# RWKV-7 head pairs in a two-layer hybrid backbone: the products of a pair made one stage later, with its solve and merge written ahead of the next pair's preparation

## The chip, the cores and the metric

The kernel runs on one core of one Trainium2 chip. The metric is the device time of one execution in microseconds; lower is better. A core has five engines that work side by side, each through its own list of instructions in order: PE (matrix products; its weight loads are shown apart, as PEld), DVE (vector), ACT (scalar), POOL and SP, the last two here mostly for issuing DMAs. They wait for each other by semaphores.

## The reference

Two layers over 512 latent tokens of width 1024, with 256 context tokens in front. The even layer runs a bidirectional RWKV-7 recurrence over 16 heads of width 64, side by side with a gated short convolution; the odd layer is a Conformer convolution module. What matters here is the recurrence, run once forward and once backward over the context and, from the states that this leaves, over the latent tokens:

```python
def step(S, inp):
    r_t, w_t, k_t, v_t, kk_t, a_t = inp
    sa = jnp.einsum("bhvk,bhk->bhv", S, -kk_t)
    S = (S * w_t[:, :, None, :]
         + sa[..., None] * (kk_t * a_t)[:, :, None, :]
         + v_t[..., None] * k_t[:, :, None, :])
    return S, jnp.einsum("bhvk,bhk->bhv", S, r_t)
...
out_f, S_f = wkv_scan(S0_f, rt, tm(decay[0]), tm(kd[0]), vt, kkt, tm(a[0]), False)
out_b, S_b = wkv_scan(S0_b, rt, tm(decay[1]), tm(kd[1]), vt, kkt, tm(a[1]), True)
```

Its output is normalised per head, a bonus term is added, and it is gated by SiLU of a projection. The short convolution is `bg * dwconv(cg * xb)`, gated as well. Both go through one output projection.

## The kernel before

Everything is float32; dense products are three float32r products of high and low parts (`mm3`, all recorded on L57). The heads are worked in eight pairs, 128 channels each. Time is cut into chunks of 64 tokens, four for the context and eight for the latent part, and the recurrence inside a chunk is turned into small matrices. For one pair (a state `st`) there are these pieces of work:

- `prep_lat` (P) loads the pair's k, v and r rows, which earlier projections left in device memory.
- `light` (L) forms decays and scaled vectors: a normalisation (`ss`, L479 to L489, with a reciprocal root of twelve tiny DVE instructions), and for each direction z a low-rank product on PE, tanh and exponentials on ACT, and the tiles AR and BK on DVE (L525 to L560). It uses the work tiles kd, a and P.
- `heavy` (H) makes the products of BK and AR on PE (`pal`, four groups of eight, each pair of banks masked into the tile E on DVE, L610), transposes BK (`pbl`), copies a part of E into `Nt` on ACT (L629), and copies v into UV (`pvl`, L640). The first product of a group waits until the group before has left its banks.
- `solve` (S) inverts the triangular blocks of E: it transposes `Nt` into X (L661), loads a unit matrix into Y, and makes 31 eliminations of two DVE instructions each (L667 and L669, tiles `xtmpl` and `Yl`).
- `merge` (M) puts the half-size inverses together: two transpositions on DVE (L675, L676), a copy into E (L680), a set of small products on PE (`uh`), a copy (L689), a second set, and a copy into E (L694). Its three work areas R1, R2 and Gs are taken from the tiles kd, a and P.
- the chain, `chain_lat`, walks the eight chunks. A step is a round trip: products of the state H with AR and of E with UV (`zol`) on PE, a copy on ACT (L769), a product with the inverse (`uh`), a copy into UV on ACT (L775), a product with BKt (`uh`), and the new state `Hl` on DVE (L782). The last of the eight steps makes no new state, so a pair has seven, `Hl_0` to `Hl_6`.
- `finish` (F) normalises a pair's output (`orq`, `po`) and stores it. `conv_branch` (C) makes the short convolution of another pair: four dense projections `pcg`, `pxb`, `pbg`, `pzb` of 24 products each, every one ahead of a weight cast on ACT and the low part on DVE (L129). The gate needs all of `pzb` and a tanh on ACT (L802).

The main loop goes over 12 stages: stages 0 to 3 run the chains of the context, stages 4 to 11 those of latent pairs 0 to 7. In every stage the chain of state s is written first, and then the letters of the table `STAGE` in their order. A letter works on the next state (O, S, M) or on the one after it (P, L, H). In the table before, the latent stages do O, S, P, L, M, H, F, C: `heavy` of a pair is written two stages ahead of its chain, its solve and merge one stage ahead, behind the next `light` for the merge.

The written order isn't the order of issue. The program goes through a scheduler that takes, among the instructions that its own time model calls ready, those written first; so work that stands later fills waits of the chain. `anchored` keeps pieces of `light` and `heavy` behind certain steps of the chain (`LIGHT_AFTER`, `HEAVY_AFTER`), and `conv_branch` has anchors of its own. The result is a fixed list per engine.

Of the kernel before, what the change touches and what calls it, by code (L numbers as in the profile page):

```python
# [15 lines left out]
P = 128  # L16
# [15 lines left out]
CONV_AFTER = (0, 2, 7, 6)  # L32
PA_ORDER = ((0, 1), (1, 0), (1, 1), (0, 0))
HEAVY = ("BAN", "ANBV")
STAGE = ("KLSMHVvF", "OPLSMHF", "OSPLMHFC")
FILL_R = (0, 0, 2, 3, 4, 4, 4, 4)
FILL_Z = (0, 1, 1, 1, 3, 3, 3, 3)
ZR = (slice(0, 64), slice(64, 128))
# [13 lines left out]
def kernel(ctx: ExitStack, tc: tile.TileContext, I: dict, out: bass.AP):  # L52
# [128 lines left out]
    def w(tag, name, dt=F32):  # L181
        return wk.tile([P, SIZE.get(tag, 512)], dt, tag=tag, name=name, bufs=NBUF.get(tag, 1))
# [470 lines left out]
    def solve(st):  # L653
        nm, E = st["nm"], st["E"]
        Xt = w("X", "X" + nm)
        X = Xt.rearrange("p (a b) -> p a b", b=32)
        Yt = w("Y", "Y" + nm)
        Y = Yt.rearrange("p (a b) -> p a b", b=16)
        tmp = w("xtmp", "xtmp" + nm)
        nc.gpsimd.dma_start(Y, I["unit"])  # L660
        V.transpose(X.rearrange("p (r s) t -> p t r s", r=2),  # L661
                    Nt.rearrange("p q t -> p t q").unsqueeze(2).to_broadcast([P, 32, 2, 16]))
        for i in range(31, 0, -1):
            c0 = i // 2
            m = 16 - c0
            tv = tmp[:, : i * m].rearrange("p (a b) -> p a b", b=m)
            V.tensor_tensor(out=tv, in0=X[:, :i, i : i + 1].to_broadcast([P, i, m]),  # L667
                            in1=Y[:, i : i + 1, c0:].to_broadcast([P, i, m]), op=ALU.mult)
            V.tensor_tensor(out=Y[:, :i, c0:], in0=Y[:, :i, c0:], in1=tv, op=ALU.add)  # L669
        st["Y"] = Y  # L670

    def merge(st):
        nm, E, Y = st["nm"], st["E"], st["Y"]
        R1, R2, Gs = (w(t, f"{t}m{nm}")[:, 0:512].rearrange("p (a b) -> p a b", b=32) for t in ("kd", "a", "P"))
        V.transpose(R1.rearrange("p q (c r) -> p c r q", r=2), Y.rearrange("p (a b) c -> p c a b", a=2))  # L675
        V.transpose(R2, R1)  # L676
        for z in range(2):
# [238 lines left out]
    sts = [prep_ctx(0, rest)]  # L916
# [15 lines left out]
    for s in range(12):  # L932
        st = sts[s]
# [7 lines left out]
            finish(st)  # L941
            break
        env["first"] = s < 4
        for x in STAGE[(s >= 2) + (s >= 4)]:
            if x == "S":
                solve(sts[s + 1])
            elif x == "M":
# [13 lines left out]
                light(sts[s + 2], st)  # L961
            elif x == "H" and s < 10:
                heavy(sts[s + 2], st)
            elif x == "F":
                fills(s + 1)
                if s >= 4:
# [47 lines left out]
    with ExitStack() as l1:  # L1014
# [182 lines left out]
        for j in range(16):  # L1197
# [5 lines left out]
            t = t2[:, j % 2 * 512 : j % 2 * 512 + 512]  # L1203
# [4 lines left out]
        for j in range(16):  # L1208
# [10 lines left out]
            t = lt("wb" if j < 10 else "xr", f"y{j}", F32R)  # L1219
# [129 lines left out]
```

## Time and profile before

| what | us |
|---|---|
| median of 3 runs (1419.38 to 1422.9) | 1421.06 |
| the profiled execution | 1428.73 |
| its span | 1426.4 |
| latent chains, first product of pair 0 to the end of pair 7 | 471.6 to 946.3 |
| from the first new state of pair 1 to that of pair 6 | 581.2 to 871.7 |

The page gives busy time per engine over the whole span; behind 946 us come the rest of the output projection and the odd layer. The stages in question are seen only by windows. A window row gives its length, then for PE, PEld, DVE, ACT and POOL the busy time with the number of instructions, the granted PE clock as a share of full speed, the share of DMA and GB/s. A row of a group gives line, engine, operation, out<-in, shapes and count, then busy time, mean ns of one, and idle time before it with what ended it. A row in the order of time gives start, length, engine, line, operation and, in brackets, the idle time before it.

### The profile page before, as it was taken

Reading aid. Unit: us, or ns where it says so; the run is one execution under the profiler, and the core shown is the slowest. Engines: PE = TensorE matmul, PEld = TensorE weight load, DVE = VectorE, ACT = ScalarE, POOL = GpSimd, SP = SyncE. Lnnn points to the kernel's source line nnn. Section 1 sums busy time; section 2 is a strip of 40 time slices with the busy share of each in tenths; the row PEclk is TensorE's granted clock in tenths of the full one; section 3 lists DMA queues with packets and bytes.
Section 4 is the critical chain, followed back from the end, with each engine's and each line's share of the span. In section 5 each row is a group of like instructions: output and inputs, shape, how many; then the busy total and the mean of one; then the engine's idle time right before and its main releaser. Section 6 shows DMA issues by size and latency. Waiting matters only on the chain.

```text
span 1426.4 us, 29742 instructions
## 1 busy us (share of the span) xinstructions
PE 1370.3 (96%) x11921; PEld 1002.7 (70%) x11921; DVE 982.2 (69%) x2294; ACT 748.5 (52%) x1516; POOL 118.2 (8%) x246
## 2 busy tenths in 40 slices
PE   6899999999999898999999999999999999999998
PEld 1474577787777676666676666768777777788886
DVE  2675597876898869999999998657745545544333
ACT  4635455535657555656666656456753323464322
POOL 2023210001011101011011100010000000000000
PEclk9999999889999999999999999999999999999999
DMA  9755432221232322232132212459813303133322
GB/s 322 226 180 160 143 121 82 64 89 59 90 101 71 112 77 68 70 100 67 56 90 70 85 47 88 130 166 323 261 40 117 119 18 101 59 104 89 103 89 89
DMA packets 137626, 158.54 MB, mean 111 GB/s; under 512 B 15375, under 2 KB 104143, under 8 KB 137369
## 3 DMA queue, kind: packets, MB, share of 16 engines
q1 hardware_dynamic: 121104, 106.47, 23.9%
q0 software_dynamic: 15312, 48.99, 10.7%
q8 instruction: 94, 1.54, 0.5%
q10 hardware_dynamic: 1072, 1.19, 0.2%
q14 instruction: 44, 0.36, 0.1%
HBM read 138.33 MB, written 18.28 MB: 110 GB/s over the span
## 4 chain that ended last, share of the span: by engine, by line
PE 52%; DVE 9%; ACT 4%; issue 2%; DMA 1%; POOL 0%; DVEq 0%; SPq 0%; ACTq 0%; POOLq 0%
PE pu L57 12%; PE pz L57 6%; PE f L57 6%; PE o L57 5%; PE zol L57 4%; PE pcg L57 3%; PE uh L57 3%; PE pxb L57 3%; DVE E L610 2%; PE pzb L57 1%; PE pc L57 1%; PE px L57 1%; PE pbg L57 1%; DVE Yl L669 1%; DVE xtmpl L667 1%
## 5 line engine op out<-in xcount | busy, mean ns | idle before, releaser
L57 PE MATMUL o<-wh,y 128*128 128x512 f32 x248 | 79.7, 397 | 0.0
L667 DVE TENSOR_TENSOR xtmpl<-Xl,Yl 128x126 f32<-128x126 f32 (+22 forms) x248 | 62.4, 252 | 3.0
L669 DVE TENSOR_TENSOR Yl<-Yl,xtmpl 128x126 f32<-128x126 f32 (+22 forms) x248 | 62.3, 251 | 2.9
L1162 ACT CAST ah<-a 64x512 fp32r<-64x512 f32 x32 | 19.8, 618 | 72.5 <-DVE a L1157 72.1
L57 PE MATMUL zol<-UV,E 64*64 64x64 f32 (+1 forms) x1024 | 54.0, 221 | 0.0
L57 PE MATMUL pal<-ARl,BKl 64*128 64x128 f32 x512 | 45.3, 296 | 7.7 <-DVE E L610 6.7
L57 PEld LDWEIGHTS o<-wh,y 128*128 128x128 f32 x248 | 45.9, 188 | 9.6
L57 PE MATMUL zol<-Hl,ARl 64*64 64x64 f32 x896 | 50.2, 230 | 1.1 <-DVE Hl L782 0.7
L775 ACT COPY UV<-uh 64x128 f32<-64x128 f32 x128 | 33.3, 260 | 32.7 <-PE uh L57 26.6
L57 PE MATMUL o<-wl,y 128*128 128x512 f32 x124 | 49.3, 398 | 0.7 <-DVE wl L129 0.7
L57 PEld LDWEIGHTS zol<-Hl,ARl 64*64 64x64 f32 x896 | 35.0, 133 | 21.3 <-issue 17.3
L57 PEld LDWEIGHTS pal<-ARl,BKl 64*128 64x128 f32 x512 | 35.6, 191 | 18.0 <-DVE E L610 6.8
L57 PEld LDWEIGHTS uh<-UV,BKt 128*64 128x64 f32 x704 | 26.3, 137 | 31.1 <-ACT UV L775 24.8
L129 DVE TENSOR_TENSOR wl<-wr,wh 128x1024 fp32r<-128x1024 f32 x28 | 34.2, 1223 | 20.2 <-ACT wh L128 20.0
L1157 DVE TENSOR_TENSOR a<-pu,a 128x512 f32<-128x512 f32 x16 | 11.0, 690 | 51.3 <-PE pu L57 49.0
L57 PEld LDWEIGHTS zol<-UV,E 64*64 64x64 f32 (+1 forms) x1024 | 42.3, 136 | 2.5 <-ACT UV L775 2.0
L610 DVE TENSOR_TENSOR E<-pal,maskE 128x512 f32<-128x512 f32 x64 | 43.2, 686 | 0.6 <-PE pal L57 0.3
L1117 DVE SCALAR_TENSOR_TENSOR pr<-px,dbe,What 119x512 f32<-119x512 f32 x32 | 22.6, 746 | 26.8 <-PE px L57 26.8
L128 ACT CAST wh<-wr 128x1024 fp32r<-128x1024 f32 x28 | 29.5, 1055 | 21.5 <-PE o L57 13.0
L57 PE MATMUL uh<-UV,BKt 128*64 128x64 f32 x704 | 36.3, 232 | 3.7 <-ACT UV L775 2.6
L886 POOL DMA_DIRECT2D mwr<-in_mod_w_dram x56 | 29.9, 537 | 114.5 <-PE uh L57 67.7
L57 PEld LDWEIGHTS uh<-Ol,E 64*64 64x64 f32 x512 | 19.9, 133 | 26.8 <-ACT Ol L769 20.4
(947 smaller groups left out, 4226.9 us busy)
## 6 DMA issues: line engine op xcount, KB each, us to landing
mwr<-in_mod_w_dram POOLq DMA_DIRECT2D x56, 256.0 KB, 3.6
wr<-in_ev_w_out_dram SPq DMA_DIRECT2D x28, 512.0 KB, 5.5
ectx<-in_mod_w_dram SPq DMA_DIRECT2D x12, 512.0 KB, 4.8
wrk<-in_ev_w_in_dram SPq DMA_DIRECT2D x16, 256.0 KB, 4.1
wrv<-in_ev_w_in_dram SPq DMA_DIRECT2D x16, 256.0 KB, 5.2
wrr<-in_ev_w_in_dram SPq DMA_DIRECT2D x16, 256.0 KB, 2.8
wrza<-in_ev_w_in_dram SPq DMA_DIRECT2D x16, 256.0 KB, 2.8
wrcg<-in_ev_w_in_dram SPq DMA_DIRECT2D x16, 256.0 KB, 2.8
```

Source lines behind the costliest of these rows:

```text
L57: return T.matmul(o, lhsT, rhs, start=start, stop=stop)
L128: S.copy(hi, raw)
L129: env["lo"].tensor_tensor(out=lo, in0=raw, in1=hi, op=ALU.subtract)
L610: st["ev"].append(V.tensor_tensor(out=E[:, h, z * NLAT + c0 : z * NLAT + c0 + m, :], in0=pas[h], in1=maskE[:, z * (1 + h) : z * (1 + h) + ...
L667: V.tensor_tensor(out=tv, in0=X[:, :i, i : i + 1].to_broadcast([P, i, m]), in1=Y[:, i : i + 1, c0:].to_broadcast([P, i, m]), op=ALU.mult)
L669: V.tensor_tensor(out=Y[:, :i, c0:], in0=Y[:, :i, c0:], in1=tv, op=ALU.add)
L775: u_ = S.copy(UV[ZR[1 - h], i : 2 * nch - i : 2 * nch - 1 - 2 * i, ZR[h]], uh[ZR[1 - h], 0:2, :])
L886: nc.gpsimd.dma_start(mws[q], I["mod_w"][layer, kt * P : (kt + 1) * P, c0 : c0 + 512])
L1117: V.scalar_tensor_tensor(out=pr[s][:NPROD], in0=px[s][:NPROD], scalar=dbe[:, 0:1], in1=What[:, n * 512 : n * 512 + 512], op0=ALU.add, op1= ...
L1157: V.tensor_tensor(out=a, in0=pp[1], in1=a, op=ALU.mult)
L1162: S.copy(ahl[s][hr], a[hr])
```

## The change

Three things change. In the latent stages `heavy` is written for the next state instead of the one after (a new letter A, first in the stage and without anchors); the stage of the last context chain loses its H, which had made pair 1's products. Solve and merge now stand ahead of P and L. And `merge` of latent pairs other than 0 takes its three work areas from the two halves of X and from Y of that pair's own solve, which are free by then, and no longer from kd, a and P.

```diff
--- before.py
+++ after.py
@@ -32,7 +32,7 @@
 CONV_AFTER = (0, 2, 7, 6)
 PA_ORDER = ((0, 1), (1, 0), (1, 1), (0, 0))
 HEAVY = ("BAN", "ANBV")
-STAGE = ("KLSMHVvF", "OPLSMHF", "OSPLMHFC")
+STAGE = ("KLSMHVvF",) * 2 + ("OPLSMHF", "OPLSMF", "AOSMPLFC")
 FILL_R = (0, 0, 2, 3, 4, 4, 4, 4)
 FILL_Z = (0, 1, 1, 1, 3, 3, 3, 3)
 ZR = (slice(0, 64), slice(64, 128))
@@ -667,11 +667,14 @@
             V.tensor_tensor(out=tv, in0=X[:, :i, i : i + 1].to_broadcast([P, i, m]),
                             in1=Y[:, i : i + 1, c0:].to_broadcast([P, i, m]), op=ALU.mult)
             V.tensor_tensor(out=Y[:, :i, c0:], in0=Y[:, :i, c0:], in1=tv, op=ALU.add)
-        st["Y"] = Y
+        st["Y"], st["Xt"], st["Yt"] = Y, Xt, Yt
 
     def merge(st):
         nm, E, Y = st["nm"], st["E"], st["Y"]
-        R1, R2, Gs = (w(t, f"{t}m{nm}")[:, 0:512].rearrange("p (a b) -> p a b", b=32) for t in ("kd", "a", "P"))
+        if st["lat"] and st["p"]:
+            R1, R2, Gs = (t.rearrange("p (a b) -> p a b", b=32) for t in (st["Xt"][:, 0:512], st["Xt"][:, 512:], st["Yt"]))
+        else:
+            R1, R2, Gs = (w(t, f"{t}m{nm}")[:, 0:512].rearrange("p (a b) -> p a b", b=32) for t in ("kd", "a", "P"))
         V.transpose(R1.rearrange("p q (c r) -> p c r q", r=2), Y.rearrange("p (a b) c -> p c a b", a=2))
         V.transpose(R2, R1)
         for z in range(2):
@@ -941,7 +944,7 @@
             finish(st)
             break
         env["first"] = s < 4
-        for x in STAGE[(s >= 2) + (s >= 4)]:
+        for x in STAGE[min(s, 4)]:
             if x == "S":
                 solve(sts[s + 1])
             elif x == "M":
@@ -961,6 +964,8 @@
                 light(sts[s + 2], st)
             elif x == "H" and s < 10:
                 heavy(sts[s + 2], st)
+            elif x == "A":
+                heavy(sts[s + 1])
             elif x == "F":
                 fills(s + 1)
                 if s >= 4:
```

What this does to the lists of instructions is shown at three places. Names carry the pair: `Hl3_0` is the state after step 0 of pair 3, `Xl4` and `Yl4` are pair 4's solve, `rnql5` and `ssl5` belong to `light` of pair 5, `pal4...` are products of pair 4.

DVE at the start of pair 3's chain, before:

```order
L782 SCALAR_TENSOR_TENSOR Hl3_0_7859<-uh0_123,PCl30_6569,HPl3_0_7831 128x64
L782 SCALAR_TENSOR_TENSOR Hl3_0_7859<-uh0_123,PCl31_6598,HPl3_0_7831 128x64
L669 TENSOR_TENSOR Yl4_8106<-Yl4_8106,xtmpl4_8107 128x23x5
L479 STREAM_TRANSPOSE rncl5_8193<-ssl5_8191 128x512
L667 TENSOR_TENSOR xtmpl4_8107<-Xl4_8105,Yl4_8106 128x110
L482 TENSOR_SCALAR rnql5_8195<-rncl5_8193 128x16
L669 TENSOR_TENSOR Yl4_8106<-Yl4_8106,xtmpl4_8107 128x22x5
L426 TENSOR_SCALAR rnql5_8195<-rnql5_8195 128x16
L667 TENSOR_TENSOR xtmpl4_8107<-Xl4_8105,Yl4_8106 128x126
L428 TENSOR_TENSOR rnql5_8195<-rnql5_8195 128x16
```

DVE in the middle of pair 3's chain, after the change:

```order
L785 SCALAR_TENSOR_TENSOR Hl3_3_7842<-uh0_123,PCl30_6640,HPl3_3_7810 128x64
L785 SCALAR_TENSOR_TENSOR Hl3_3_7842<-uh0_123,PCl31_6669,HPl3_3_7810 128x64
L610 TENSOR_TENSOR E100_4148<-pal4001_8017,maskE_107 128x512
L610 TENSOR_TENSOR E100_4148<-pal4000_8016,maskE_107 128x512
L785 SCALAR_TENSOR_TENSOR Hl3_4_7877<-uh0_123,PCl30_6640,HPl3_4_7845 128x64
L785 SCALAR_TENSOR_TENSOR Hl3_4_7877<-uh0_123,PCl31_6669,HPl3_4_7845 128x64
L798 TENSOR_TENSOR Ol3_7712<-zol3_4_7853,Ol3_7712 128x128
L661 STREAM_TRANSPOSE Xl4_8096<-Nt_111 128x32x32
L785 SCALAR_TENSOR_TENSOR Hl3_5_7912<-uh0_123,PCl30_6640,HPl3_5_7880 128x64
L785 SCALAR_TENSOR_TENSOR Hl3_5_7912<-uh0_123,PCl31_6669,HPl3_5_7880 128x64
L798 TENSOR_TENSOR Ol3_7712<-zol3_5_7888,Ol3_7712 128x2x64
L667 TENSOR_TENSOR xtmpl4_8098<-Xl4_8096,Yl4_8097 128x31
```

Before, solve steps of pair 4 and the normalisation of pair 5 stand between the new states of pair 3's chain from its first step on. Now the masks of pair 4's products and the transposition stand there, and the first solve step of pair 4 comes behind `Hl3_5`. From `Hl3_0` to `Hl3_3` there is nothing but states and masks either.

DVE at the end of the merge of pair 4, after the change:

```order
L692 COPY Yl4_8097<-uh1_124 32x512
L827 SCALAR_TENSOR_TENSOR bonl3_6624<-po3_8352,hcol_77,bonl3_6624 128x512
L861 TENSOR_TENSOR yb4_8451<-pbg4_8467,yb4_8451 128x512
L828 SCALAR_TENSOR_TENSOR bonl3_6624<-bonl3_6624,hcol_77,gz3_8369 128x512
L129 TENSOR_TENSOR wlcg50_9202<-wrcg50_9200,whcg50_9201 128x512
L697 COPY E100_4148<-uh1_124 32x16x32
L129 TENSOR_TENSOR wlcg51_9208<-wrcg51_9206,whcg51_9207 128x512
L129 TENSOR_TENSOR wlxb50_9241<-wrxb50_9239,whxb50_9240 128x512
L806 SCALAR_TENSOR_TENSOR gzb4_8530<-gzb4_8530,pzb4_8505 128x512
L864 TENSOR_TENSOR yb4_8451<-yb4_8451,gzb4_8530 128x512
L785 SCALAR_TENSOR_TENSOR Hl4_0_8563<-uh0_123,PCl40_7466,HPl4_0_8535 128x64
```

The last copy of the merge (L697, which was L694) now stands five rows ahead of pair 4's first new state. Before, 36 DVE rows of other work stood between the two.

PE at the same place, after the change:

```order
L57 MATMUL pbg4_8467<-hlh_117,whbg41_8462 128x512
L57 MATMUL pbg4_8467<-hll_118,whbg41_8462 128x512
L57 MATMUL pbg4_8467<-hlh_117,wlbg41_8463 128x512
L57 MATMUL uh1_124<-Xl4_8096,Yl4_8097 32x32 x32
L57 MATMUL pzb4_8505<-hlh_117,whzb40_8494 128x512
L57 MATMUL pzb4_8505<-hll_118,whzb40_8494 128x512
L57 MATMUL pzb4_8505<-hlh_117,wlzb40_8495 128x512
```

The row with `Yl4` is the second product of pair 4's merge. It is followed by all 24 products of `pzb4`, of which the first three are shown, and then by the first products of pair 4's chain. Before, the second product of the merge stood among `pal` products, ahead of the last of `pbg4`, of all of `pzb4`, and of the transposes and `po` and `pv` products.

## The prediction

> **What bounds the kernel now.** I read the page first, then the busy time by windows, the groups of instructions on DVE and ACT in one window, and the order of time for single steps. Line numbers are those of the kernel before; in the changed file lines from 675 on stand 3 later, in the main loop up to 5.
>
> ```profile
> PE 1370.3 (96%) x11921; PEld 1002.7 (70%) x11921; DVE 982.2 (69%) x2294; ACT 748.5 (52%) x1516; POOL 118.2 (8%) x246
> ```
>
> By the page PE is the limit. But 69% for DVE is a mean over the program. The windows below are cut at the first new state (`Hl`, L782) of a pair's chain, which stands once per pair and step:
>
> ```profile
> 517.07 0.47 DVE L782 SCALAR_TENSOR_TENSOR Hl<-uh,PCl,HPl 128x64 f32<-128x64 f32 x2
> 581.16 0.44 DVE L782 SCALAR_TENSOR_TENSOR Hl<-uh,PCl,HPl 128x64 f32<-128x64 f32 x2
> 871.73 0.48 DVE L782 SCALAR_TENSOR_TENSOR Hl<-uh,PCl,HPl 128x64 f32<-128x64 f32 x2
> core 0: us, PE busy (x) PEld busy (x) DVE busy (x) ACT busy (x) POOL busy (x), PEclk, DMA share, GB/s
> 464.00:517.10 53.10, 48.24 (x448) 37.47 (x446) 39.48 (x84) 24.16 (x45) 4.52 (x9) 1.00 0.36 105
> 517.10:581.20 64.10, 58.96 (x779) 42.02 (x777) 58.55 (x179) 37.16 (x89) 7.48 (x14) 0.95 0.24 72
> 581.20:871.70 290.50, 278.77 (x3856) 196.24 (x3855) 268.77 (x776) 187.75 (x444) 29.14 (x54) 1.00 0.25 74
> 871.70:916.00 44.30, 44.19 (x640) 31.32 (x634) 31.57 (x97) 19.23 (x56) 2.06 (x4) 1.00 0.19 59
> 696.50:721.50 25.00, 24.38 (x347) 16.43 (x345) 23.36 (x79) 19.18 (x53) 1.24 (x3) 1.00 0.21 62
> 721.50:754.50 33.00, 31.16 (x429) 22.98 (x426) 30.73 (x80) 18.31 (x36) 5.50 (x10) 1.00 0.28 86
> ```
>
> The third window row holds the five equal stages of pairs 1 to 5: 290.5 / 5 = 58.1 us each, with PE busy 96% and DVE 93% (268.8 of 290.5). Two engines are nearly full at once. This works because DVE always has something else to do while the chain of pair p waits: the last two rows cut one stage (pair 3) at the last `Hl`, and DVE is busy 23.4 of 25.0 us during the chain and 30.7 of 33.0 after it. A change that empties DVE in one of these parts must pay in the other.
>
> **The change part by part.** No arithmetic is added or removed: the products, masks, solve steps and merges are the same in number, on the same engines. What changes is when they stand, and each engine works its list in order. So I walk one stage of the changed order with durations of this trace.
>
> ```profile
> L610 DVE TENSOR_TENSOR E<-pal,maskE 128x512 f32<-128x512 f32 x8 | 5.3, 684 | 0.0
> L782 DVE SCALAR_TENSOR_TENSOR Hl<-uh,PCl,HPl 128x64 f32<-128x64 f32 x14 | 3.3, 278 | 1.0 <-PE uh L57 0.5 <-ACT sg L514 0.4
> L661 DVE STREAM_TRANSPOSE Xl<-Nt 128x1024 f32<-128x1024 f32 x1 | 2.0, 1996 | 0.1
> L525 DVE TENSOR_TENSOR_SCAN Pl<-scm,sg 128x528 f32<-128x528 f32 x2 | 2.5, 1258 | 0.5 <-ACT sg L517 0.5
> L667 DVE TENSOR_TENSOR xtmpl<-Xl,Yl 128x56 f32<-128x56 f32 x2 | 0.4, 212 | 0.0
> L629 ACT COPY Nt<-E 32x512 f32<-32x512 f32 x4 | 2.5, 617 | 0.1
> L640 ACT COPY UV<-pvl 64x512 f32<-64x512 f32 x4 | 2.3, 582 | 0.8 <-PE pvl L57 0.8
> L57 PE MATMUL pal<-ARl,BKl 64*128 64x128 f32 x64 | 5.9, 293 | 0.0
> ```
>
> *DVE during the chain.* Before, 77 to 80 instructions stand between the first and the last `Hl` of a pair, 32 to 35 of them solve steps (L667, L669). Now 34 stand there: 14 `Hl` (3.3 us), 6 masks (L610, 6/8 of 5.3 = 4.0), two O sums (0.6), the transposition L661 (2.0), ten short solve steps (0.2 each) and one cast (0.7). That is 12 us with the small overlaps taken off. The solve can't start before `heavy` of the same pair has given E and ACT has copied it into Nt, and `light` of the pair after stands behind the solve. So of a stage's 54 us of DVE work (268.8 / 5), 42 now stand behind the last `Hl`, where 31 stood.
>
> *How long the chain part takes.* A step is a round trip:
>
> ```profile
> 638.86 0.43 DVE L782 SCALAR_TENSOR_TENSOR Hl<-uh,PCl,HPl 128x64 f32<-128x64 f32 x2
> 639.44 0.45 PE L57 MATMUL zol<-Hl,ARl 64*64 64x64 f32 x8
> 639.69 0.43 PE L57 MATMUL zol<-UV,E 64*64 64x64 f32 x8
> 640.18 0.27 ACT L769 COPY Ol<-zol 128x128 f32<-128x128 f32 x1 [0.26 <-PE zol L57]
> 641.21 0.53 ACT L775 COPY UV<-uh 64x128 f32<-64x128 f32 x2 [0.77 <-PE uh L57]
> 641.79 0.45 PE L57 MATMUL uh<-UV,BKt 128*64 128x64 f32 x8
> 696.53 0.47 DVE L782 SCALAR_TENSOR_TENSOR Hl<-uh,PCl,HPl 128x64 f32<-128x64 f32 x2
> 699.98 0.48 DVE L782 SCALAR_TENSOR_TENSOR Hl<-uh,PCl,HPl 128x64 f32<-128x64 f32 x2
> ```
>
> Adding the pieces gives 3.3 us; 696.53 to 699.98 is a step of 3.45, and the six of that pair took 25.0. An emptier DVE can't shorten it much. In the changed order four steps go at about 3.5; one waits 0.4 for masks that free a bank of the next products; and the fifth has three Nt copies (3 x 0.62) ahead of its `Ol` copy on ACT and then the transposition (2.0) ahead of its `Hl` on DVE: 5.2. The sum is 4 x 3.5 + 3.9 + 5.2 = 23. That saves 2, not the 11 us of DVE work that left.
>
> *Behind the last `Hl`.* 42 us of DVE work in list order, and these waits: the three pv copies (3 x 0.58) stand on ACT ahead of the last step's UV copy and delay the product that `light` begins with (1); a dozen solve steps stand back to back instead of between independent ones (1); the scans and exponentials of `light`, whose ACT work now follows that late product instead of running beside the chain (1.5; the scans wait 0.5 today); the merge's first product before the copy L689 (1). Then the end:
>
> ```profile
> 676.27 1.20 PE L57 MATMUL uh<-aml,E 32*32 32x32 f32 x64 [0.52 <-DVE aml L676]
> 679.39 1.20 PE L57 MATMUL uh<-kdml,Pml 32*32 32x32 f32 x64
> 907.97 0.39 PE L57 MATMUL pzb<-hlh,wlzb 128*128 128x512 f32 x1
> 912.76 0.39 PE L57 MATMUL pzb<-hlh,wlzb 128*128 128x512 f32 x1
> L802 ACT ACTIVATE gzb<-pzb 128x512 f32<-128x512 f32 x1 | 0.6, 599 | 0.0
> ```
>
> Now the merge's second product is followed on PE by all 24 `pzb` products, and only then by the next chain. From 907.97 to 912.76 there are 21 of them: 0.228 each, so 24 take 5.5. DVE has casts for 2.5 us of that and then waits 3 for `gzb` (pzb, then 0.6 of tanh on ACT); the next `Hl` comes a chain's first step after `pzb` (1 more of waiting). Sum: 42 + 4.5 + 4 = 50.5, and with the chain part 73.5 us for a stage.
>
> *The clock.* PE's work of a stage is unchanged (55.8 busy), so it now stands idle some 18 us per stage. About 10 of them come in one piece: `pbg` needs the cast of `wlbg` (L129), which is the 85th DVE instruction behind the last `Hl`, some 29 us on, while the products listed ahead of `pbg` fill about 18. The trace has one place with such waits:
>
> ```profile
> 551.20 1.16 PE L57 MATMUL pal<-ARl,BKl 64*128 64x128 f32 x16 [1.67 <-DVE E L610]
> 554.57 2.08 PE L57 MATMUL pal<-ARl,BKl 64*128 64x128 f32 x16 [2.21 <-DVE E L610]
> 557.17 0.63 PE L57 MATMUL pbg<-hlh,whbg 128*128 128x512 f32 x1
> 557.59 0.63 PE L57 MATMUL pbg<-hll,whbg 128*128 128x512 f32 x1
> 553.40:560.20 6.80, 5.63 (x29) 4.27 (x31) 6.47 (x27) 2.47 (x4) 0.00 (x0) 0.50 0.28 80
> ```
>
> After two waits of 1.67 and 2.21 us the granted clock is 0.50 for 6.8 us: the same 16 products take 2.08 instead of 1.16, the dense ones 0.42 apart instead of 0.228. Behind `pbg` this is covered, since PE then waits again for DVE; in the merge and `pzb` it isn't. I take 2.5 us per stage: both merge products at the ratio of those two (0.9 + 0.9), and a third of `pzb` (8 x 0.19 = 1.5), three times in four. The Trainium skill has a rule on this ("TensorE: Matmul & The Clock Gate", section "HAM oscillation — how this bites in real kernels"): PE gaps longer than about 3.4 us put the array back to half clock and must be avoided. The trace agrees and shows it at shorter gaps still; by the page's window a gap costs 1.7 us, an estimate, and two per stage would make the term 3.4 instead of 2.5.
>
> So a stage is 73.5 + 2.5 = 76 us, against 58.1: five of them give 5 x 17.9 = +90.
>
> *The ends.* Ahead of pair 0's first `Hl` (464.0 to 517.1, PE 48.2 busy) all but one of pair 1's 32 products (the `pal` row, 5.9), its transposes and eight masks leave: about 8 us of PE work and 2 of the 4.9 us of idle, -10 (between -12 and -5). Pair 0's own stage has 158 instructions on DVE instead of 177, but 135 of them (48 us) behind the last `Hl`; its end is shorter, with one `pzb` product behind the merge: 23 + 48 + 5 = 76 against 64.1, +12. Pair 6 has no `light` after it: 92 instructions (31 us) and 52 solve steps mostly back to back give 23 + 33 = 56 against 44.3, +12; but 17 more of the output projection's products stand ahead in that wait (4 us), so +8. Pair 7's chain stays.
>
> *Buffers and queues.* `merge` now writes halves of X and Y instead of kd, a and P; same widths, no cost, and covered by nothing because it needs no cover. POOL's list keeps its order of loads but for the v load, now behind a store and ahead of gz; v is read in step 6 of the next chain, some 20 us on: zero, or up to 2 per stage if it were late.
>
> Sum: -10 + 12 + 90 + 8 = +100. The profiled execution took 1428.73 (span 1426.4), 7.7 above the median of the runs; the difference is carried over to the median: 1421 + 100 = **1521 us**.
>
> **The rivals.** *A milder loss (0.20):* the chain steps all at 3.45 (20.7), DVE with few waits (42 + 4), no clock loss: 67 per stage, 5 x 9 + 5 + 2 - 12 = +40: 1461. For it: DVE lost only 7% to waits before. Against: the 5.5 us of `pzb` between merge and chain stand in the list whatever else happens. *Half clock over the whole chain (0.15):* a chain step's 1.6 us of products at 1.8 times their length, all of `pzb` and both merges: 8 x 1.2 + 4.8 + 1.8 = +16 per stage on 73.5: 157 + 25 + 15 - 8 = +189, 1610; half of it 1565. For it: dense products fill the chain's waits today, and most leave; and one stretch at half clock has PE busy throughout:
>
> ```profile
> 276.90:297.40 20.50, 20.50 (x203) 16.96 (x195) 8.00 (x11) 4.70 (x8) 0.05 (x1) 0.50 0.11 37
> ```
>
> Against: the chains of pairs 1 to 5 all ran at 1.00 (the third window row). *No change (0.03):* PE decides and DVE's list has room, 1421. Against: 42 us of list behind the chain do not fit into 33. *Faster (0.04):* `light` and `merge` no longer share kd, a and P, so the merge comes earlier and PE's waits close: (290.5 - 278.8) + 10 = 22 us at most, 1399; it decides if PE's idle time, not DVE's list, stands before each chain. That the move isn't made can be excluded: the order shows it, but for one group of products in four that stays in the earlier stage.
>
> **How the numbers follow.** My forecast has 0.58. The range 1470 to 1565 leaves out half of the milder case, a third of the clock case, and both cases of no loss: 0.2. A measurement of this kernel tells 0.3% (4 us) from no change: faster 0.04, same 0.03, slower 0.93.
>
> **What would show it.** Right: 75 us from first `Hl` to first `Hl` for pairs 1 to 5; DVE busy under 15 of some 23 us in the chain part and over 40 behind it; PE idle before `pbg`, released by DVE L129; granted clock under 0.95. Wrong: DVE's solve steps inside the early chain steps, or stages below 62 us.

## The result, and the profile after

| | median us | executions |
|---|---|---|
| before | 1421.98 | 1419.38 to 1423.65 |
| after | 1504.12 | 1501.14 to 1506.58 |

The change makes the kernel slower: ratio 1.0578, 95% interval 1.0551 to 1.0606. That is 82 us, where 100 had been forecast (1521, range 1470 to 1565).

The profiled execution of after took 1501.14 us (span 1498.9). From the page of after, first the busy times of PE and DVE, then the group with the longest wait on PE:

```profile
PE 1374.2 (92%) x11921; PEld 1019.9 (68%) x11921; DVE 987.2 (66%) x2294; ACT 753.5 (50%) x1516; POOL 118.2 (8%) x246
L57 PE MATMUL pbg<-hlh,wlbg 128*128 128x512 f32 x64 | 31.5, 493 | 57.2 <-DVE wlbg L129 57.2
```

The work is the same: 11921 products, 2294 DVE instructions, and busy times of PE, DVE, ACT and POOL that differ by at most 0.7% (PEld: 1.7%). What is new above all is 57.2 us in which PE waited for one kind of DVE cast.

The windows of after, cut at its own `Hl` (now L785): from the last context state to pair 0's first `Hl`; the stage of pair 0; the five stages of pairs 1 to 5; the stage of pair 6; then pair 3's stage in its two parts, up to the last `Hl` and behind it; then two stretches for the clock (the column ahead of the last two is the granted clock):

```profile
core 0: us, PE busy (x) PEld busy (x) DVE busy (x) ACT busy (x) POOL busy (x), PEclk, DMA share, GB/s
454.60:497.40 42.80, 39.38 (x335) 31.70 (x334) 32.20 (x74) 17.19 (x32) 4.47 (x9) 1.00 0.45 127
497.40:571.30 73.90, 61.24 (x794) 44.98 (x790) 56.72 (x159) 39.06 (x89) 6.36 (x12) 0.91 0.21 62
571.30:933.70 362.40, 291.73 (x3864) 217.02 (x3859) 274.98 (x781) 190.24 (x444) 30.45 (x55) 0.91 0.20 58
933.70:991.90 58.20, 56.22 (x761) 42.43 (x757) 44.02 (x127) 30.03 (x74) 2.69 (x5) 1.00 0.29 93
714.50:737.50 23.00, 22.32 (x385) 16.20 (x383) 11.95 (x33) 14.06 (x43) 0.54 (x1) 1.00 0.08 25
737.50:787.40 49.90, 35.97 (x398) 27.12 (x394) 43.06 (x126) 24.08 (x46) 6.17 (x11) 0.86 0.27 76
756.60:770.30 13.70, 3.78 (x9) 3.01 (x10) 13.24 (x42) 3.87 (x8) 3.44 (x6) 0.50 0.40 115
276.90:297.40 20.50, 20.50 (x278) 17.08 (x277) 14.17 (x31) 10.22 (x18) 0.83 (x2) 1.00 0.25 77
```

A stage of pairs 1 to 5 takes 362.4 / 5 = 72.5 us instead of 58.1. In the chain part DVE is busy 11.95 of 23.0 us (before 23.4 of 25.0), behind the last `Hl` 43.06 of 49.9 (before 30.7 of 33.0). That is the loss: 11.4 us of DVE's work have gone from one side of the last `Hl` to the other. The side that lost the work became only 2 us shorter; the other became 16.9 us longer, 12.3 of them work and 4.6 waits of DVE.

The times add up: 42.8 against 52.8 from the last context state to pair 0's first `Hl` (before: 464.3 to 517.1; -10.0), 73.9 against 64.1 (+9.8), 362.4 against 290.5 (+71.9), 58.2 against 44.3 (+13.9), and 3.4 us less in pair 7's chain and behind it: +82.2, as the medians say. The two profiled executions differ by only 72.4, since that of before had 20.5 us at half clock in the context part (shown in the prediction), where the last row shows 1.00.

The order of time in pair 3's chain, DVE only, four of its rows:

```profile
718.39 0.48 DVE L785 SCALAR_TENSOR_TENSOR Hl<-uh,PCl,HPl 128x64 f32<-128x64 f32 x2 [1.45 <-PE uh L57]
726.08 0.48 DVE L785 SCALAR_TENSOR_TENSOR Hl<-uh,PCl,HPl 128x64 f32<-128x64 f32 x2 [3.20 <-PE uh L57]
731.96 2.03 DVE L661 STREAM_TRANSPOSE Xl<-Nt 128x1024 f32<-128x1024 f32 x1 [1.82 <-ACT Nt L629]
737.45 0.47 DVE L785 SCALAR_TENSOR_TENSOR Hl<-uh,PCl,HPl 128x64 f32<-128x64 f32 x2
```

DVE now waits in the chain for the chain's own products (1.45, 3.20) and for the copy of the masked products; the solve's transposition comes at 731.96, one and a half steps ahead of the last `Hl`. Then the same stage's end, PE, ACT and DVE:

```profile
755.43 1.16 PE L57 MATMUL pal<-ARl,BKl 64*128 64x128 f32 x16 [2.27 <-ACT BKl L561]
766.52 0.79 PE L57 MATMUL pbg<-hlh,wlbg 128*128 128x512 f32 x1 [9.93 <-DVE wlbg L129]
774.67 1.20 PE L57 MATMUL uh<-Xl,E 32*32 32x32 f32 x64
777.66 1.20 PE L57 MATMUL uh<-Xl,Yl 32*32 32x32 f32 x64
781.68 0.62 ACT L128 CAST whcg<-wrcg 128x512 fp32r<-128x512 f32 x1 [2.20 <-PE pzb L57]
782.34 0.69 DVE L129 TENSOR_TENSOR wlcg<-wrcg,whcg 128x512 fp32r<-128x512 f32 x1 [1.75 <-ACT whcg L128]
785.05 0.69 DVE L129 TENSOR_TENSOR wlxb<-wrxb,whxb 128x512 fp32r<-128x512 f32 x1 [2.02 <-ACT whxb L128]
787.38 0.48 DVE L785 SCALAR_TENSOR_TENSOR Hl<-uh,PCl,HPl 128x64 f32<-128x64 f32 x2 [0.19 <-PE uh L57]
```

PE waits 9.93 us for the cast of `wlbg` and then has `pbg`, the merge and all of `pzb` before the next chain. DVE's two waits behind the merge (1.75 and 2.02) are for casts on ACT (`whcg`, `whxb`) that in turn wait for `pzb`, whose weights still hold the buffers: there are three for such half weights.

### The profile page after: what moved, and what is told of

Read it like the earlier page. It is cut to its first block, busy times and chain, and to the rows that moved or that the text cites. A ratio compares the mean times of both kernels' runs of the same rounds, so it can differ in the third digit from the quotient of the medians.

```text
span 1498.9 us, 29754 instructions
## 1 busy us (share of the span) xinstructions
PE 1374.2 (92%) x11921; PEld 1019.9 (68%) x11921; DVE 987.2 (66%) x2294; ACT 753.5 (50%) x1516; POOL 118.2 (8%) x246
## 3 DMA queue, kind: packets, MB, share of 16 engines
q0 software_dynamic: 15312, 48.99, 10.3%
## 4 chain that ended last, share of the span: by engine, by line
PE 37%; DVE 7%; ACT 3%; DMA 2%; issue 1%; DVEq 0%; SPq 0%; ACTq 0%
PE pu L57 12%; PE pz L57 6%; PE f L57 6%; PE o L57 3%; PE zol L57 2%; PE uh L57 2%; PE pzb L57 1%; PE pc L57 1%; PE px L57 1%; PE pcg L57 1%; PE pal L57 1%; DMA wr<-in_ev_w_out_dram 1%; DVE Yl L669 1%; DVE xtmpl L667 1%; DMA wrzb<-in_ev_w_in_dram 1%
## 5 line engine op out<-in xcount | busy, mean ns | idle before, releaser
L57 PE MATMUL pbg<-hlh,wlbg 128*128 128x512 f32 x64 | 31.5, 493 | 57.2 <-DVE wlbg L129 57.2
L57 PE MATMUL pal<-ARl,BKl 64*128 64x128 f32 x512 | 62.9, 311 | 14.0 <-ACT BKl L561 13.4
L57 PEld LDWEIGHTS pal<-ARl,BKl 64*128 64x128 f32 x512 | 41.8, 187 | 26.9 <-ACT BKl L561 16.0
L785 DVE SCALAR_TENSOR_TENSOR Hl<-uh,PCl,HPl 128x64 f32<-128x64 f32 x112 | 26.5, 277 | 48.3 <-PE uh L57 27.9
L57 PEld LDWEIGHTS pbg<-hlh,wlbg 128*128 128x128 f32 x64 | 15.2, 237 | 62.0 <-DVE wlbg L129 58.5
L1167 ACT CAST ah<-a 64x512 fp32r<-64x512 f32 x32 | 19.8, 619 | 72.5 <-DVE a L1162 72.1
L57 PE MATMUL o<-wl,y 128*128 128x512 f32 x124 | 49.9, 403 | 1.7 <-DVE wl L129 1.6
L1162 DVE TENSOR_TENSOR a<-pu,a 128x512 f32<-128x512 f32 x16 | 11.0, 690 | 51.2 <-PE pu L57 48.9
L129 DVE TENSOR_TENSOR wl<-wr,wh 128x1024 fp32r<-128x1024 f32 x28 | 34.2, 1222 | 16.0 <-ACT wh L128 15.8
```

The source lines that it names most:

```text
L57: return T.matmul(o, lhsT, rhs, start=start, stop=stop)
L129: env["lo"].tensor_tensor(out=lo, in0=raw, in1=hi, op=ALU.subtract)
L785: h_ = V.scalar_tensor_tensor(out=Hn[:, z, :], in0=uh[:, 2 + z, :], scalar=PC[z][:, i : i + 1], in1=HP[:, z, :], op0=ALU.mult, op1=ALU.add)
L1162: V.tensor_tensor(out=a, in0=pp[1], in1=a, op=ALU.mult)
L1167: S.copy(ahl[s][hr], a[hr])
```

## The experiments

The theory: each engine works its list in order; with `heavy` one stage later the solve can't fill the chain's waits, and `light`, listed among the solve's steps, can't either, so the stage is chain plus DVE's list behind it. The rivals: the buffers, the length of the path from masks over solve to merge, PE's wait before `pbg`, the half clock. Where a run of a changed kernel is set against after, the times of the kernel before, 1419.8 to 1422.0 in every set of runs, show that the sets compare.

### Which part of the change

The change has three parts. One does nothing by itself: with the new buffers, the tables `OSPLMHFC` and `OSMPLHFC` (merge behind or ahead of P and L) give the same list on every engine but for buffer numbers, and so do `AOSPLMFC` and `AOSMPLFC`. The other two were taken apart.

**Buffers alone** (e1): the changed kernel with

```diff
-STAGE = ("KLSMHVvF",) * 2 + ("OPLSMHF", "OPLSMF", "AOSMPLFC")
+STAGE = ("KLSMHVvF",) * 2 + ("OPLSMHF", "OPLSMHF", "OSPLMHFC")
```

> The changed kernel with the old stage table, so that only the buffers of merge differ from the kernel before: it works in halves of X and in Y instead of kd, a and P. My theory (the late place of heavy on DVE's list costs everything): 1421 us, within 5 of the kernel before. Rival 1 (kd, a and P come free earlier for light, and that is worth something): 1400 to 1412. Rival 2 (the new buffers hold up the next solve, since its unit matrix is loaded into Y only when merge is done): the 82 us of the change or part of it show here, 1440 to 1500.

Measured: 1422.56 us, ratio 1.0018 (0.9985 to 1.0051): no change. Its five stages of pairs 1 to 5, by windows:

```profile
571.90:862.90 291.00, 278.80 (x3861) 197.06 (x3860) 269.63 (x781) 188.82 (x445) 29.63 (x53) 1.00 0.25 75
```

291.0 against 290.5. The buffers neither help nor hurt where `heavy` stands early.

**The table alone** (e2): the changed kernel with

```diff
-        if st["lat"] and st["p"]:
+        if False:
```

> The changed kernel with its new stage table, but merge in kd, a and P as before. light of the next pair writes kd, a and P too, so it now stands behind merge on every engine; the projections of the conv branch move ahead of it. DVE has 113 instructions behind the last Hl instead of 121 of the changed kernel and 76 of the one before. My theory (heavy's late place decides, not the buffers): as slow as the change, 1505 us, between 1485 and 1540; the wait of light for exponentials lies open (some 3 us per stage more), the 24 pzb products before the chain don't (4 less). Rival (the buffers cause the loss): 1421 to 1440.

Measured: 1543.61 us, ratio 1.0825 (1.0769 to 1.0881), just above the range given. The loss belongs to the table, and the new buffers recover about 40 us of it. Windows: the chain part of pair 2, the same of pair 3, and the stretch around the latter:

```profile
655.40:678.10 22.70, 21.20 (x388) 15.54 (x384) 11.90 (x37) 14.05 (x43) 0.18 (x1) 1.00 0.09 29
731.00:765.60 34.60, 34.41 (x406) 24.87 (x404) 13.51 (x41) 15.29 (x46) 0.00 (x0) 0.58 0.05 16
709.00:760.20 51.20, 39.27 (x409) 29.54 (x409) 27.53 (x62) 19.60 (x52) 5.63 (x10) 0.50 0.11 35
```

Here the prediction's clock rival is seen at work: 51.2 us at half clock, and a chain of 34.6 us instead of 22.7. It befell two of the eight latent chains in this execution (12 us each), so 24 of the 40 us are the clock. PE was busy 34.41 of those 34.60 us, with small products, and the clock came back only at 760.2, 29 us into the chain.

**Light behind the conv branch, with the new buffers** (e7) shows whether e2 lost by the wait for kd, a and P or by the order that it brings:

```diff
-... "AOSMPLFC")
+... "AOCSMPLF")
```

> The changed kernel (merge in X and Y) with the table AOCSMPLF: the conv branch is written ahead of solve and merge, so that it and not light stands between the solve steps, and light follows behind merge. This is nearly the order of the run with the old buffers, where the wait for kd, a and P had put light behind merge; DVE has 113 instructions behind the last Hl in both. Theory (the buffers matter only by the order that they allow): as slow as that run, 1543, between 1525 and 1555, with chains of pairs at half clock again. Rival (the wait for the buffers itself costs): 1490 to 1510.

Measured: 1553.73 us (three executions at 1549.6 to 1556.9, one at 1577.6), ratio 1.0933 (1.0891 to 1.0975). It is 10 us slower than e2 without any such wait, so the order is what counts. PE, behind the last `Hl` of pair 1, by time:

```profile
654.67 2.08 PE L57 MATMUL pal<-ARl,BKl 64*128 64x128 f32 x16 [7.91 <-ACT al L521]
663.51 1.61 PE L57 MATMUL pal<-ARl,BKl 64*128 64x128 f32 x10 [6.75 <-DVE orq L426]
```

The window of pair 1's chain:

```profile
582.90:618.70 35.80, 35.63 (x405) 25.75 (x402) 13.64 (x41) 15.22 (x46) 0.00 (x0) 0.54 0.06 18
```

With `light` behind the merge little other work is left beside its exponentials, and PE waits 7.91 and 6.75 us for it in this stage (in the next four the same within 0.02); pair 1's chain is again at half clock: 35.8 us.

### What it is in heavy's late place

**Light first** (e3): `heavy` stays late, but DVE gets other work for the chain.

```diff
-... "AOSMPLFC")
+... "AOPLSMFC")
```

> The changed kernel with the last stage's table AOPLSMFC instead of AOSMPLFC: heavy stays one stage late, but light of the pair after is written ahead of the solve, so that DVE has light's work for the chain's waits: 76 of its instructions stand between the first and the last Hl (34 in the changed kernel, 80 before), 79 behind. My theory (what costs is DVE's in-order list, empty in the chain and full behind it): stages of 58 to 63 us, 1420 to 1450, 1435 at best guess. Rival (masks, copies, transposition, solve and merge of a pair need their time one after the other inside one stage, wherever the list has them): stages stay at 70 or more, 1490 to 1510.

Measured: 1451.87 us, ratio 1.0214 (1.0184 to 1.0244), just above the theory's range and 52 us below after. The five stages of pairs 1 to 5, and pair 2's in its two parts:

```profile
581.60:892.50 310.90, 285.52 (x3877) 210.48 (x3875) 275.71 (x786) 187.30 (x449) 30.79 (x55) 0.94 0.24 70
645.70:671.30 25.60, 24.60 (x382) 16.69 (x380) 23.54 (x78) 21.55 (x59) 1.08 (x2) 1.00 0.10 28
671.30:707.40 36.10, 31.71 (x397) 25.11 (x397) 31.96 (x84) 16.05 (x33) 5.68 (x10) 0.89 0.34 101
```

DVE is busy 23.54 of 25.6 us in the chain again and a stage is 62.2 us. So filling DVE's chain part again took back three quarters of the stage's loss (10.3 of 14.4 us). The other 4.1 us were not taken apart; about 36 of these 310.9 us ran at half clock. The path from masks to merge inside one stage doesn't need 70 us; that rival fell.

**The price of DVE work** (e9, e10): in both kernels, behind line 541,

```diff
+                for _ in range(4 if 2 <= st["p"] <= 7 else 0):
+                    V.tensor_tensor(out=bon, in0=bon, in1=bon, op=ALU.max)
```

> The changed kernel with four more DVE instructions in light of pairs 2 to 7, each the maximum of bon with itself (128x512, some 0.66 us from start to start), so work without use: 2.6 us more DVE work per stage, behind the last Hl, in the stages of pairs 0 to 5. It isn't on the path from masks over solve to merge, and no product waits for it. My theory (DVE's list behind the last Hl is the stage): it is paid in full, 6 x 2.6 = 16 us: 1520, between 1514 and 1526. Rival (the path masks, solve, merge, or PE's late pbg, sets the stage, and DVE's 6 us of waits per stage take it up): 1502 to 1508.

> The kernel before with the same four DVE instructions in light of pairs 2 to 7. There DVE is busy 93% and PE 96% of a stage. My theory (both lists are nearly full, PE's a little more): DVE's 4 us of waits per stage take up some of it, half is paid: 1429, between 1424 and 1435. Rival 1 (PE alone is the bound): 1421. Rival 2 (DVE's list is the bound before too): 1437 or more.

Measured: after with it 1521.39 us, 17.3 more than after (ratio to before 1.0707, 1.0681 to 1.0733). Before with it 1442.77, 22 more (1.0176, 1.0139 to 1.0212). Of after with the added work first the group of `pbg` from the page, then windows over its five stages and over pair 3's part behind the last `Hl`:

```profile
L57 PE MATMUL pbg<-hlh,wlbg 128*128 128x512 f32 x64 | 32.8, 513 | 74.8 <-DVE wlbg L129 74.8
```

Windows of the same kernel:

```profile
576.40:954.80 378.40, 295.48 (x3866) 219.75 (x3860) 286.35 (x801) 190.36 (x444) 30.51 (x56) 0.88 0.20 56
749.70:801.90 52.20, 36.45 (x400) 27.58 (x396) 45.45 (x130) 24.18 (x46) 6.23 (x12) 0.84 0.26 73
```

And before with the added work: its five stages, then of these the stages of pairs 2 and 3 and those of pairs 4 and 5:

```profile
577.20:880.50 303.30, 286.30 (x3857) 201.97 (x3855) 278.78 (x788) 187.47 (x444) 29.23 (x53) 0.97 0.24 71
635.80:761.70 125.90, 118.92 (x1555) 84.48 (x1551) 113.66 (x322) 75.84 (x179) 14.28 (x26) 0.95 0.24 71
761.70:880.50 118.80, 112.68 (x1541) 79.30 (x1539) 110.87 (x313) 74.59 (x177) 8.95 (x17) 0.99 0.24 71
```

In after the 16 us of useless work are paid in full, and a little more (16.0 us in the five stages, for 13; the half clock lasts 17.1 us in a stage instead of 13.7, which may be a part of it): the part behind the last `Hl` grows to 52.2, and PE's wait for `wlbg` from 57.2 to 74.8. In before the sum is as high (12.8 us in the five stages), where the theory had given half, but it doesn't show the same thing. 10.3 of the 12.8 us lie in the stages of pairs 2 and 3 (115.6 us without the added work), in each of which PE ran 6.8 us at half clock behind waits of 1.46 and 1.03 us; the five stages of before ran at full clock throughout. PE is busy 118.9 us in those two stages instead of 111.3, with the same products. The three other stages cost 2.5 us for 7.8 us of added work. So the price in before came largely with the half clock, which set in behind PE's waits for DVE; that DVE's list as such was the limit there isn't shown.

### The terms behind the last Hl

**Conv ahead of merge** (e4), against the 24 `pzb` products between merge and chain:

```diff
-... "AOSMPLFC")
+... "AOSPLCMF")
```

> The changed kernel with the last stage's table AOSPLCMF: the conv branch is written ahead of merge, so that the 24 pzb products stand ahead of the merge's first product on PE instead of between its second and the next chain; DVE has 117 instructions behind the last Hl instead of 121. My theory (those products cost 4 us of every stage, 24 over six stages): 1480 us, 1474 to 1488, with stages of 68 to 69 us for pairs 1 to 5. Rival (they are hidden behind casts that DVE has to make anyway): 1500 to 1506.

Measured: ratio 1.0616 (1.0563 to 1.0668), executions from 1503.1 to 1517.7 us (one far longer execution, 4142 us, is left out). No gain, where the theory had 1480. In the profiled execution the chain of pair 4 ran 16.5 us at half clock, and its stage took 78.6 us; the stages of pairs 1, 2, 3 and 5 took 71.3 on average, in after 72.1, so the 4 us are missing without it too. The stage's end of pair 3:

```profile
771.32 0.79 PE L57 MATMUL pbg<-hlh,wlbg 128*128 128x512 f32 x1 [8.79 <-DVE wlbg L129]
780.18 0.85 DVE L683 COPY E<-Xl 32x512 f32<-32x512 f32 x2
784.37 1.20 PE L57 MATMUL uh<-Xl,E 32*32 32x32 f32 x64
788.36 1.20 PE L57 MATMUL uh<-Xl,Yl 32*32 32x32 f32 x64 [0.83 <-DVE Yl L692]
794.00 0.48 DVE L785 SCALAR_TENSOR_TENSOR Hl<-uh,PCl,HPl 128x64 f32<-128x64 f32 x2 [1.35 <-PE uh L57]
```

The price only changed its place: merge's copy is done at 781.03, but its first product stands behind all of `pzb` and starts at 784.37, 3.3 us later. From `pbg`'s start to the next `Hl` it is 22.7 us, against 20.9 in after.

**The bg casts on POOL** (e5), to let `pbg` run in PE's wait:

```diff
 def lo_for(nm):
-    env["lo"] = V
+    env["lo"] = G if nm in ("bg1", "bg2", "bg3", "bg4", "bg5", "bg6") else V
```

> The changed kernel with the two wlbg casts of pairs 1 to 6's conv branch (line 129, bg weights) on POOL instead of DVE; nothing else changes place by hand. The casts then wait only for their weights, pbg's 24 products stand right behind pxb in PE's wait, 19 of the 24 pzb products come ahead of the merge's first product, and one is left between merge and chain. My theory (DVE's list releases pbg some 10 us late, and behind pbg PE has too much left before the chain): 1.4 us of DVE work and 4 to 5 us at the end of a stage go, 5.5 to 6.5 us in each of six stages: 1468 us, 1460 to 1478, PE's 9.9 us wait before pbg gone. Rival 1 (DVE's list alone decides, PE's wait costs nothing): 1.4 us each, 1495. Rival 2 (PE's wait is the loss): the whole 9.9 us each, 1445.

Measured: 1487.41 us, ratio 1.0480 (1.0446 to 1.0514): 17 us less than after, between the theory and its first rival. A group from its page:

```profile
L57 PE MATMUL pzb<-hlh,wlzb 128*128 128x512 f32 x64 | 32.6, 510 | 48.4 <-DVE wlzb L129 48.4
```

The window of the five stages of pairs 1 to 5:

```profile
573.10:918.50 345.40, 290.06 (x3850) 215.37 (x3844) 277.82 (x768) 189.56 (x444) 45.63 (x66) 0.92 0.21 61
```

A stage is 69.1 us, 3.4 less. PE's wait for the bg cast is gone and has reappeared, 48.4 us in six stages, before `pzb`, at the next cast in DVE's list. So PE's wait before `pbg` was a shadow of DVE's list: freeing that product group brought 3.4 us, not the 9.9 us of the wait. The 1.4 us of DVE work per stage were not won: twelve DVE instructions, seven of them solve steps, were held beside the POOL casts and took 12.7 us longer in all than in after (what holds them is under e8), so DVE was busy 277.8 us in the five stages instead of 275.0. What was won are DVE's waits, 67.6 us instead of 87.4, or 4.0 a stage. That is what the theory had for the end of a stage, where most `pzb` products now come ahead of the merge. The held instructions are most of the 19 us that are missing to 1468.

**Filler products** (e6), against the half clock. Ahead of the real products of `pbg`:

```diff
+            for k in range(28 if 0 < p < 7 else 0):
+                mm(pbg, wt[0][0][:, 0:P], hlat[0][:, k % KT, :], True, True)
             proj(wt, pbg, hlat)
```

> The changed kernel with 28 dense products more ahead of each pbg of pairs 1 to 6, written to pbg's own bank and overwritten by pbg's first product: work without use, 28 x 0.228 = 6.4 us of PE's waits of 2.3 us (before pal) and 9.9 us (before pbg). They keep PE busy where the granted clock fell to 0.50 in every stage; the order of everything else stays. My theory (the half clock lies under PE's wait for DVE and costs nothing): no change, 1504, between 1499 and 1509, even where the 13.7 us stretches at 0.50 go or shrink. Rival (the half clock costs the 2.5 us of a stage that the prediction put down for it): 1489 where the stretches go. If the stretches stay, this run says nothing on it.

Measured: 1495.40 us (1493.58 to 1502.34), ratio 1.0532 (1.0504 to 1.0560): 9 us faster than after, with more work, below the range given for the theory. By windows: the stages of pairs 3 to 5, those of pairs 1 and 2, and one stretch at half clock:

```profile
718.60:935.60 217.00, 195.25 (x2406) 147.21 (x2402) 165.12 (x470) 113.86 (x266) 16.66 (x30) 0.95 0.20 58
582.00:718.60 136.60, 123.90 (x1592) 94.17 (x1588) 108.28 (x310) 76.56 (x178) 12.91 (x23) 0.96 0.22 63
769.30:776.10 6.80, 5.49 (x13) 4.38 (x14) 6.53 (x26) 1.85 (x3) 0.85 (x2) 0.50 0.39 112
```

The order of time, two rows of pair 2's end and two of pair 3's:

```profile
702.38 0.79 PE L57 MATMUL pbg<-hlh,wlbg 128*128 128x512 f32 x1 [4.13 <-DVE wlbg L129]
718.65 0.47 DVE L785 SCALAR_TENSOR_TENSOR Hl<-uh,PCl,HPl 128x64 f32<-128x64 f32 x2
770.61 0.80 PE L57 MATMUL pbg<-hlh,wlbg 128*128 128x512 f32 x1 [5.95 <-DVE wlbg L129]
790.71 0.48 DVE L785 SCALAR_TENSOR_TENSOR Hl<-uh,PCl,HPl 128x64 f32<-128x64 f32 x2 [0.18 <-PE uh L57]
```

Two things are mixed here, and for pairs 0 to 2 the order is not what the expectation says. For pairs 3 to 5 the list but for the fillers is that of after, and the stretch at half clock is 6.8 instead of 13.7 us: a stage is 72.3 instead of 73.1 (after: 714.5 to 933.7 over three). So 7 us less at half clock are worth some 0.7 us here. For pairs 1 and 2 the fillers led the scheduler to another list, with all `pzb` products ahead of merge's second product, and one `wlbg` cast earlier: 68.3 us a stage instead of 71.6. There the end from `pbg` to the next `Hl` is 16.3 us, against 20.1: this is the 4 us that the prediction put down for `pzb`, and e4 missed. Most of the 9 us come from there (2 x 3.3 against 3 x 0.7), not from the clock, as far as the two can be told apart: the stretches at half clock became shorter in pairs 1 and 2 as well.

### Towards a better kernel

**Casts on POOL in the kernel before** (e8):

```diff
 def lo_for(nm):
-    env["lo"] = V
+    env["lo"] = G if nm[:2] in ("bg", "cg") and nm[2:] not in ("0", "7") else V
```

> The kernel before with the wlbg and wlcg casts of pairs 1 to 6 on POOL (8% busy) instead of DVE (93% busy in the stages): four of the eight casts of a stage, 4 x 0.69 = 2.7 us of DVE's 54. Theory (PE is 96% busy there, so at most its 2.3 us per stage can be won, and DVE's in-order list is what causes them): 1410 to 1420, 1416 at best guess. Rival (a cast on POOL takes some us, and late casts hold up pbg): 1425 to 1450.

Measured: 1435.79 us, ratio 1.0101 (1.0064 to 1.0138): 1% slower, as the rival had it. In the order of time, a cast on POOL and the solve step beside it on DVE, then another POOL cast and a DVE instruction during it:

```profile
654.06 1.42 POOL L129 TENSOR_TENSOR wlbg<-wrbg,whbg 128x512 fp32r<-128x512 f32 x1 [12.93 <-ACT whbg L128]
654.24 1.36 DVE L669 TENSOR_TENSOR Yl<-Yl,xtmpl 128x110 f32<-128x110 f32 x1
724.38 4.06 POOL L129 TENSOR_TENSOR wlbg<-wrbg,whbg 128x512 fp32r<-128x512 f32 x1 [0.56 <-ACT whbg L128]
725.90 0.68 DVE L555 SCALAR_TENSOR_TENSOR ARl<-kkl,Pl 128x512 f32<-128x512 f32 x1
```

The window over its five stages of pairs 1 to 5:

```profile
579.90:883.50 303.60, 285.76 (x3870) 200.23 (x3866) 284.23 (x770) 188.63 (x446) 57.99 (x73) 0.98 0.24 71
```

The step of 0.25 us took 1.36, and ended 0.1 us behind the cast. The last two rows show the other direction: DVE's instructions, listed close behind each other, ran at their usual length (0.68), and the cast took 4.06 us. Fifteen of 496 latent solve steps took over 0.6 us, every one beside a POOL cast; in before and after none took over 0.31. By that window DVE is busy 284.2 us, 15 more than before, with 14 us of casts less. The Trainium skill ("SBUF — State Buffer", section "Who interferes with whom") says that a DVE instruction with two inputs in SBUF and a GpSimd instruction that reads SBUF exclude each other, and that the order of issue decides which of them waits; the cast and the DVE instructions above read two tiles each, and the trace agrees in both pairs of rows.

**Merge's copies on ACT in the kernel before** (e11 two of them, e12 four), after e10 had put 22 us on 16 us of DVE work there:

```diff
-            (V.tensor_copy if z else S.copy)(Gs[low[z]], ch3(pg[low[z]], 32))
+            (V.tensor_copy if z and not onact else S.copy)(Gs[low[z]], ch3(pg[low[z]], 32))
...
-            (V.tensor_copy if z else S.copy)(E[top[z], 1 - z, :, 32:64], ch3(px[top[z]], 32))
+            (V.tensor_copy if z and not onact else S.copy)(E[top[z], 1 - z, :, 32:64], ch3(px[top[z]], 32))
```

with `onact` true for latent pairs 1 to 7; e12 does the same to the copy of line 680.

> The kernel before with two of merge's copies for latent pairs 1 to 7 (the halves z = 1 of lines 689 and 694, 0.69 us each) on ACT instead of DVE, on top of ACT's own two: 1.4 us less DVE work in each of seven stages, 1.2 more on ACT, which is 65% busy there. My theory after the added DVE work cost 22 us for 16 us of it (DVE's list bounds the kernel before too): 7 x 1.4 = 10 us less, 1411, between 1405 and 1415. Rival (merge's later copies hold up its second product and the next chain, or PE is the bound): 1418 to 1428.

> The same, and also the two copies of line 680 that DVE makes (0.42 us each): 2.2 us less DVE work in each of seven stages, 2.4 more on ACT, all of it on merge's own path (four copies one after the other instead of two beside two). My theory: 7 x 2.2 = 15 us less, 1405, between 1398 and 1412. Rival (ACT's list, which carries the chain's copies too, is now late): 1418 to 1435.

Measured: e11 1415.79 us, ratio 0.9963 (0.9934 to 0.9991); e12 1421.67, ratio 1.0008 (0.9980 to 1.0037). The five stages of pairs 1 to 5, of e11 first:

```profile
571.30:856.80 285.50, 280.26 (x3862) 197.01 (x3860) 265.24 (x766) 193.20 (x455) 29.77 (x54) 1.00 0.26 76
```

and of e12:

```profile
572.20:866.00 293.80, 280.79 (x3864) 198.41 (x3862) 265.36 (x761) 199.46 (x465) 29.73 (x54) 0.99 0.25 74
```

e11 is the fastest of all kernels here, by a little: 57.1 us a stage, with PE busy 98% of it, so that PE may now be the limit, which no run tested; its median lies just above the range given. e12 takes more work off DVE and gains nothing: DVE is busy as long as in e11 but stands idle 8 us more. In these stages it waits longer for ACT's copy `Nt` ahead of the transposition (3.7 us instead of 0.4) and for PE at the masks (4.5 instead of 0.2), so with four copies of the merge on ACT, ACT's own list seems to come late, as the rival had it.

## Why the prediction was right

It was right in direction and range, and in where the time goes. 18 us of its 100 were too much, nearly all in the five equal stages, and there mostly in the term for the clock.

- *What bounds.* That DVE's list, empty in the chain and full behind it, is what a stage of the changed kernel rests on is shown by e3 and e9. For the kernel before the prediction said that both engines are nearly full; e10 doesn't decide between them, since its cost came largely with the half clock.
- *DVE in the chain:* 34 instructions and 12 us were worked out; the window counts 33 and 11.95 us. *The chain part:* 23 us worked out, 23.0 measured for pair 3 (22.2 to 23.3 over pairs 0 to 6). The single steps came otherwise, between 3.2 and 4.5 us, and only their sum was right, which is luck in part.
- *Behind the last `Hl`:* 50.5 worked out as 42 of work and 8.5 of waits; 49.9 measured in pair 3, as 43.06 and 6.8. The 4 us for `pzb` are there (1.75 and 2.02), but not as a wait for `gzb`: DVE waits for casts on ACT which `pzb` holds up. Another 1.31 us of its waits there are for the cast of `whzb` on ACT, which itself had waited 1.90 us for the load of its weights; the prediction has no such wait. e5 and e6 show the 4 us for `pzb` removable (4.0 and 3.8 us), e4 that moving the conv branch bodily doesn't remove them.
- *The clock, the step that failed:* 2.5 us per stage, for merge and `pzb` at half clock. The half clock did come, 13.7 us in every stage of pairs 0 to 5, but in the stages of pairs 1 to 5 it began at most 2 us into the wait before `pbg` and ended 4 to 6 us behind that wait, so merge and `pzb` ran at full clock, and e6 puts some 0.7 us on half of it. In pair 3's stage DVE's waits were 1.7 us less than worked out and its work 1.1 more; on average a stage took 72.5 us instead of 76, which is +71.9 for pairs 1 to 5 instead of +90.
- *The ends:* -10 ahead of pair 0 was -10.0; +12 for pair 0 was +9.8; +8 for pair 6 and behind was +13.9 - 3.4 = +10.5.
- *The moved v load and the new buffers,* costed at nothing: in the five stages of after no wait for the v load shows, and e1 bears out the buffers. e2 shows what they are for: with the new table and the old buffers, `light` would stand behind the merge, and the loss would be half as large again.
- *The rivals.* The milder loss (67 us a stage) and the gain didn't come. Half clock over the whole chain didn't come in after, where every chain ran at 1.00; e2 and e7 show that it was near, at 12 to 13 us for each chain, more than the 8 x 1.2 us taken for it.
- *What would show it:* stages of 75 us (72.5), DVE under 15 of 23 us in the chain (11.95) and over 40 behind it (43.06), PE idle before `pbg` for DVE L129 (9.9 us in each of these stages), a clock under 0.95 (0.91): all seen, the first with a smaller number.

## What to carry to other kernels

Where two engines are both above 90% busy in a stage, ask of a move not how much work it shifts but from which wait it takes the work away: here the same instructions, taken out of the chain's waits and put behind it, cost 72 us in five stages. A long wait of the other engine (9.9 us before `pbg`) can be only the shadow of the full list: releasing it made it reappear at the next item. What a us of an engine's work costs can be measured by adding useless work of that kind. In the changed kernel the answer was plain; in the one before most of the price came with stretches at half clock, so the clock has to be read stage by stage beside the time. It still pointed to the one version that beat both kernels, though by 6 us only.

## What the runs showed of the hardware

- The granted clock fell to 0.50 behind PE waits of 2.0 to 2.3 us among small products, at most 2 us into the next wait (before: behind 1.67 us, during the next wait, of 2.21; e10: behind 1.46 and 1.03). PE busy with a chain's small products didn't bring it back for 29 us in e2 (from 731.0) and 33 us in pair 1's chain of e7 (from 582.9). The Trainium skill ("TensorE: Matmul & The Clock Gate", section "HAM oscillation — how this bites in real kernels") speaks of gaps over about 3.4 us; the lengths at half clock seen here (3.4, 6.8, 13.7, 20.5) are multiples of that, but the waits ahead of them were shorter. Behind the start of dense products the clock came back after 3.7 to 5.6 us in the six stages of after (pair 3: `pbg` from 766.5, full clock from 770.3).
- A chain of the same products takes 22.7 us at full clock and 34.6 at 0.58: half clock costs a chain 12 us, though its steps are round trips over three engines.
- A cast on POOL with two inputs (mostly 1.3 to 1.7 us) held the DVE solve step beside it until it ended: in e8 15 steps of some 0.25 us took 0.6 to 1.4. Where DVE's instructions followed each other closely, the cast was held instead and took 3.2 and 4.1 us.
